# A hybrid decoder layer in fp32: other places in SBUF for up blocks' weights and for some activations

## The chip, the core and the metric

The kernel runs on one core of a Trainium2 chip. The metric is the time on the device in microseconds (us); each number of "runs" is a median over executions that were timed one by one. One further execution was profiled, and all rows shown come from it. The engines are TensorE (PE in the rows; its weight loads are PEld), VectorE (DVE), ScalarE (ACT), GpSimd (POOL) and SyncE (SP), which issues the weight DMAs. SBUF is the on-chip memory from which all of them read.

## The reference

One post-norm decoder layer on 256 tokens plus 16 meta tokens, width 2048, all in fp32. Cut to what matters here:

```
p   = h @ w_in                              # q heads, shared latent, indexer, pool channels
mix = concat(attention(p), pooling(p)) @ w_o
h   = LN(alpha * h + mix)
z   = h @ w_up                              # 2048 -> 2 x 5632
a, g = split(causal depthwise conv (width 3) of z)
h   = LN(alpha * h + (gelu(a) * g) @ w_down) # 5632 -> 2048
```

Nearly all of the work is in the four products with `w_in`, `w_o`, `w_up` and `w_down`.

## The kernel before

**Three products for one.** TensorE multiplies operands in the type fp32r. To keep fp32's precision each fp32 operand is cut into an upper and a lower part, and each matmul is done as three: upper weight by upper activation (L288), and the two mixed ones (L292, in a loop). With weights of 128 x 128 and activations of 128 x 258 (256 tokens and two more that the convolution wants) a block of 128 output columns takes 16 K steps of three matmuls. `product` (L281 to 292) is this loop. The order of the two mixed matmuls is `turned` (weight's lower part first) or not.

**The weight stream.** All weight tiles of 128 x 2048 go through one stream (L158 on): `w_in` (tiles `in_w_proj`), the latent's two tiles, `w_o` (16 tiles), then the tiles of the FFN in the order that `ffn_plan` writes down: an up tile and a down tile by turns, 88 up and 80 down, the four last down tiles at the end. The up blocks are numbered b = 2f + half, where half 0 is the value and half 1 the gate of column block f. The first 8 of them work on activations into which LayerNorm is folded (`fold`, 260 columns wide with two extra), the other 80 on normalised activations `hp`, made by `normalise` (L799 to 808). The FFN has six parts of columns; from the second part on a down tile of the part before follows each up tile. A down tile of `seven` (L890 to 892) computes 4 or 3 of the seven products of a 2 x 2 Strassen scheme, kind A or B by turns, with activations `gp` and `right`.

**From DMA to TensorE.** For a tile, `fetch` issues the DMA on SP's queue into a raw tile `wraw`; then `split_part` makes the upper part by a copy on ScalarE (L181) and the lower part by a subtraction on VectorE (L182), both into the tile `whl`. This is done in pieces, given by `cuts`: (0, 1024, 2048), or (0, 512, 2048) where the tile has a lead. A tile of kind A or B has one or three more subtractions on VectorE (L193 to 199). `wraw` and `whl` have three buffers each, and tiles are fetched two ahead of their use. VectorE and ScalarE also do the convolution (L821 to 823), the gate (L838, L839) and the activations' splits, in an order that a scheduler sets from the program's order and its own model; `issue_after` adds edges to it.

**Where the parts stand.** `Split` (L68 to 82) is the layout of a `whl` tile: the upper part at one offset, the lower at another, in elements of 4 bytes. With a **lead**, the first 512 columns (the first four K steps) stand elsewhere: their upper part at the lead's offset, the lower part 576 further on, and the rest behind. `places` and `WAYS` give offsets and turn by position in the stream; `LEAD_X` is the lead of eight tiles of the input projection, `LEAD_H` = (12, False) that of three tiles of `w_o` and of all up tiles (`lead(b)`). Tiles of `w_o` without a lead stand at 0 and 2048, turned; an up tile has this too for the part behind its lead. `Parts` (L85 to 92) is the layout of an activation tile: `xp` (input) at 0 and 274, `hp` at 2 and 276, `fold` at 32 and 304. `K_UP` is the order of K steps in an up block; its first entry is K tile 1.

Of the kernel before, what the change touches and what calls it, by code (L numbers as in the profile page):

```python
# [12 lines left out]
F32R = mybir.dt.float32r  # L13
# [4 lines left out]
P = 128  # L18
# [3 lines left out]
T = NM + S  # L22
Q0 = NM - 2
NQ = T - Q0
# [43 lines left out]
class Split:  # L68

    def __init__(self, tile, upper, lower, turned=False, lead=None, early=False):

        self.tile, self.places, self.turned, self.lead, self.early = tile, (upper, lower), turned, lead, early

    def __getitem__(self, key):
        rows, part, c = key
        o = self.places[part]
        if self.lead is not None:
            assert c.stop <= LEAD or c.start >= LEAD  # L80
            o = self.lead + (LEAD + 64) * part if c.stop <= LEAD else self.places[0] + LEAD + 128 + (2048 - LEAD) * part
        return self.tile[rows, o + c.start:o + (2 * 1024 + 2 if c.stop is None else c.stop)]


# [9 lines left out]


WIDE = 288
LEAD = 512
WAYS = (10, 2048, False), (12, 2048, True), (0, 2048, True), (0, 2048, True)


LEAD_X, LEAD_H = (24, False), (12, False)


def lead(b):

    return LEAD_H


GATED, RIGHT, FOLD = 0, 32, 32
# [20 lines left out]
K_UP = (1, 3, 5, 7, 8, 10, 12, 15, 0, 2, 4, 6, 9, 11, 13, 14)  # L130
# [3 lines left out]
def tile_layer(ctx, tc, xt, w_first, w_proj, w_uk, w_uv, w_pool, w_o, w_up, w_down, cols, rows, rel_bias, onehot, out):  # L134
# [3 lines left out]
    ring = ctx.enter_context(tc.tile_pool(name="ring", bufs=24))  # L138
# [21 lines left out]
    for item in plan:  # L160
# [3 lines left out]
        elif item[0] == "down":  # L164
            n = PARTS[FAST]
# [19 lines left out]
    def fetch(raw, hl, src, kind, front):  # L185

        nc.sync.dma_start(raw, src)
        b11, b12, b21, b22 = (raw[:, c:c + 512] for c in range(0, 2048, 512))
        cuts = (0, 1024, 2048)
        if kind == "A":  # L190

            with tc.issue_after(front):
                nc.vector.tensor_tensor(b12, b12, b11, op=ALU.subtract)  # L193
        if kind == "B":

            with tc.issue_after(front):
                nc.vector.tensor_tensor(b12, b22, b12, op=ALU.subtract)  # L197
            nc.vector.tensor_tensor(b11, b12, b11, op=ALU.add)  # L198
            nc.vector.tensor_tensor(b21, b21, b11, op=ALU.subtract)
            cuts = (0, 1024, 1536)  # L200
        if hl.lead is not None:
            cuts = (0, LEAD, 2048)
        for a, b in zip(cuts, cuts[1:]):
            parts = split_part(raw, hl, slice(a, b))
        return parts
# [75 lines left out]
    def product(ps, hl, act, lo, hi, places, ks=None, k0=0, k1=KT):  # L281

        for n in range(k0, k1):
            k = (places if ks is None else ks)[n]
            w = slice(P * places.index(k), P * places.index(k) + P)
            wh, wl = hl[:, 0, w], hl[:, 1, w]
            ah, al = act[k][:, 0, lo:hi], act[k][:, 1, lo:hi]
            nc.tensor.matmul(ps, wh, ah, start=n == 0, stop=False)  # L288
            turned = hl.early if hl.lead is not None and w.start < LEAD else hl.turned
            turn = ((wl, ah), (wh, al)) if turned else ((wh, al), (wl, ah))  # L290
            for i, (a, b) in enumerate(turn):
                nc.tensor.matmul(ps, a, b, start=False, stop=i == 1 and n == KT - 1)  # L292
# [6 lines left out]
    for k0, k1 in [(k, k + 1) for k in range(9)] + [(9, 12), (12, 15), (15, 16)]:  # L299
        if k0 == KT - 1:  # L300

            raw = ap_.tile([P, 1024], F32, name="wraw_l", tag="v1")[:, :T + MF].rearrange("p (a b) -> p a b", a=1)
        elif k0 % 3 == 0:
            raw = wp.tile([P, 2048], F32, tag="wraw", name="wraw")
            raw = raw[:, :3 * (T + MF)].rearrange("p (a b) -> p a b", b=T + MF)
        if k0 % 6 == 0:
            hl = split_tile()
        for w in ((slice(0, T), slice(T, T + MF)) if k0 == 0 else (slice(0, T + MF),)):
            nc.sync.dma_start(raw[:, k0 % 3:k0 % 3 + k1 - k0, w], w_first[k0:k1, :, w].rearrange("k p c -> p k c"))
        for k in range(k0, k1):  # L310
            xk, wk, a0 = raw[:, k % 3, :T], raw[:, k % 3, T:], k % 6 // 3 * 1024 + k % 3 * MF
            c = slice(a0, a0 + MF)
            a = Parts(ring.tile([P, 2, WIDE], F32R, tag="act", name="xp"), 0, T)
            nc.scalar.activation(a[:, 0, :], xk, AF.Copy)
            nc.scalar.activation(hl[:, 0, c], wk, AF.Copy)
            nc.vector.tensor_tensor(a[:, 1, :], xk, a[:, 0, :].bitcast(F32), op=ALU.subtract)
            nc.vector.tensor_tensor(hl[:, 1, c], wk, hl[:, 0, c].bitcast(F32), op=ALU.subtract)
            x_parts.append(a)
            first.append((hl, c.start))
# [480 lines left out]
    def normalise(m):  # L800
# [1 line left out]
        nc.vector.tensor_tensor(yd, yd, rs, op=ALU.mult)  # L802
        nc.vector.tensor_tensor(yd, yd, m2, op=ALU.add)
        nc.scalar.activation(yd, yd, AF.Identity, bias=col(LN1, 2 * m + 1), scale=col(LN1, 2 * m))
        a = Parts(ring.tile([P, 2, WIDE], F32R, tag="act", name="hp"), 2, NQ)
        nc.scalar.activation(a[:, 0, :NQ], yd, AF.Copy)
        nc.vector.tensor_tensor(a[:, 1, :NQ], yd, a[:, 0, :NQ].bitcast(F32), op=ALU.subtract)
        h_parts.append(a)
# [191 lines left out]
    n = PARTS[-1]  # L1000
# [189 lines left out]
```

## Time and profile before

| what | value |
|---|---|
| median of 3 runs | 1026.68 us (1025.87 to 1028.61) |
| profiled execution | 1027.44 us |
| its span, from the first to the last instruction | 1025.6 us |
| TensorE busy, share of the span | 99% |
| VectorE, ScalarE, GpSimd busy | 87%, 60%, 18% |
| HBM read | 232.50 MB |
| the granted clock of TensorE | 0.997 of full speed |

A group of instructions is told by its line, engine, operation, and the tiles written and read (out<-in); x is a count. Behind the busy time a group's row has the mean duration in ns, then the idle time of the engine ahead of the group and what ended it. A timeline's row has a start in us from the span's begin, a duration in us, and the instruction. Matmuls are pipelined: a next one may start before the one ahead of it ends, so that how long a block takes is read from starts and not from durations. The chain that ended last is followed back from the last instruction, at each step to what released it.

### The profile page before, as it was taken

The page shows a single profiled execution, that of the slowest core. Times are in us where ns is not written, and L with a number is a line of the kernel's source. Part 1 is how long each engine was busy: PE and PEld are TensorE (multiplying, and loading weights), DVE is VectorE, ACT ScalarE, POOL GpSimd, SP SyncE. Part 2 cuts the span into 40 slices and gives each one's busy share as a digit, 9 for nine tenths or more (in the row PEclk, how much of TensorE's full clock was granted, in tenths as well). Part 3 has the DMA queues.
Part 4 walks back from the last instruction along what each step waited for, and adds up shares of the span by engine and source line. Part 5 has one row for each costly group of instructions (what it writes and reads, how often), then busy time and mean ns, then how long its engine had stood idle before and what let it go on. Part 6 is the DMA issues. An engine that isn't in the chain of part 4 may idle for free.

```text
span 1025.6 us, 19201 instructions
## 1 busy us (share of the span) xinstructions
PE 1018.5 (99%) x7644; PEld 969.4 (95%) x7644; DVE 890.5 (87%) x1401; ACT 620.1 (60%) x1000; POOL 188.4 (18%) x245
## 2 busy tenths in 40 slices
PE   9999999999999999999999999999999999999997
PEld 8999999999999999999999999999999999999986
DVE  6878668758879998999998989989899999999876
ACT  7666446645448856555666565566556656666675
POOL 1200014125430131111121111210212102120031
PEclk9999999999999999999999999999999999999998
DMA  8755643455564578979887788888888789788874
GB/s 328 257 184 206 228 154 108 138 197 168 203 205 134 189 229 249 278 283 296 281 288 259 270 275 278 277 279 298 278 272 279 292 295 289 266 290 286 290 244 138
DMA packets 59754, 250.28 MB, mean 244 GB/s; under 512 B 21734, under 2 KB 22416, under 8 KB 32656
## 3 DMA queue, kind: packets, MB, share of 16 engines
q1 hardware_dynamic: 34592, 230.42, 62.8%
q0 software_dynamic: 7888, 16.14, 8.3%
q10 hardware_dynamic: 17184, 2.49, 1.5%
q8 instruction: 60, 0.98, 0.4%
q14 instruction: 30, 0.25, 0.1%
HBM read 232.50 MB, written 2.11 MB: 229 GB/s over the span
## 4 chain that ended last, share of the span: by engine, by line
PE 71%; DVE 12%; DMA 8%; issue 4%; ACT 4%; POOL 1%; POOLq 0%; ACTq 0%; SPq 0%; DVEq 0%
PE mm L292 36%; PE mm L288 18%; DVE whl L182 6%; DMA wraw<-in_w_up 4%; DMA wraw<-in_w_down 4%; ACT whl L181 3%; PE at L891 3%; PE at L892 3%; PE at L890 3%; PE mm L363 2%; DVE y L900 1%; DVE wraw L198 1%; DVE wraw L197 1%; DVE gp L845 0%; DVE wraw L193 0%
## 5 line engine op out<-in xcount | busy, mean ns | idle before, releaser
L182 DVE TENSOR_TENSOR whl<-wraw,whl 128x1024 fp32r<-128x1024 f32 (+2 forms) x416 | 488.3, 1201 | 53.8 <-ACT whl L181 52.4
L181 ACT ACTIVATE whl<-wraw 128x1024 fp32r<-128x1024 f32 (+2 forms) x416 | 402.4, 1015 | 192.8 <-DVE wraw L198 52.1
L292 PE MATMUL mm<-hp,whl 128*128 128x258 f32 x2560 | 454.0, 280 | 0.0
L292 PEld LDWEIGHTS mm<-hp,whl 128*128 128x128 f32 x2560 | 390.9, 188 | 3.5 <-DVE whl L182 0.2
L288 PE MATMUL mm<-hp,whl 128*128 128x258 f32 x1280 | 357.6, 279 | 0.0
L288 PEld LDWEIGHTS mm<-hp,whl 128*128 128x128 f32 x1280 | 241.4, 189 | 3.1
L292 PE MATMUL mm<-xp,whl 128*128 128x256 f32 (+5 forms) x768 | 140.4, 282 | 0.0
L292 PEld LDWEIGHTS mm<-xp,whl 128*128 128x128 f32 x768 | 118.7, 189 | 0.5
L288 PE MATMUL mm<-xp,whl 128*128 128x256 f32 (+5 forms) x384 | 111.9, 292 | 0.0
L863 POOL TENSOR_TENSOR forms<-za 128x128 f32<-128x128 f32 x20 | 20.3, 1015 | 297.5 <-DVE za L839 234.5
L288 PEld LDWEIGHTS mm<-xp,whl 128*128 128x128 f32 x384 | 72.3, 188 | 1.0 <-issue 0.5
L891 PE MATMUL at<-whl,gp 128*128 128x512 f32 x180 | 70.7, 393 | 0.0
L892 PE MATMUL at<-whl,gp 128*128 128x512 f32 x180 | 70.6, 393 | 0.0
L890 PE MATMUL at<-whl,gp 128*128 128x512 f32 x180 | 68.8, 392 | 0.3 <-DVE u L914 0.3
L866 POOL TENSOR_TENSOR forms<-za 128x128 f32<-128x128 f32 x20 | 20.2, 1010 | 202.3 <-DVE za L839 190.2
L821 ACT ACTIVATE z<-mm,cv 128x256 f32<-128x256 f32 x40 | 22.3, 559 | 42.5 <-PE mm L292 42.2
L292 PE MATMUL mm<-fold,whl 128*128 128x260 f32 x256 | 45.6, 280 | 0.0
L292 PE MATMUL mm<-mixp,whl 128*128 128x258 f32 x256 | 45.5, 279 | 0.0
L292 PE MATMUL mm<-mixa,whl 128*128 128x258 f32 x256 | 45.2, 278 | 0.0
L821 ACT ACTIVATE za<-mm,cv 128x256 f32<-128x256 f32 x40 | 22.3, 558 | 35.0 <-PE mm L292 33.8
L892 PEld LDWEIGHTS at<-whl,gp 128*128 128x128 f32 x180 | 33.8, 188 | 7.4
L890 PEld LDWEIGHTS at<-whl,gp 128*128 128x128 f32 x180 | 33.5, 187 | 7.2 <-DVE u L914 1.0
(339 smaller groups left out, 1610.1 us busy)
## 6 DMA issues: line engine op xcount, KB each, us to landing
wraw<-in_w_up SPq DMA_DIRECT2D x88, 1024.0 KB, 5.2
wraw<-in_w_down SPq DMA_DIRECT2D x80, 1024.0 KB, 6.5
wraw<-in_w_proj SPq DMA_DIRECT2D x24, 1024.0 KB, 5.2
wraw<-in_w_o SPq DMA_DIRECT2D x16, 1024.0 KB, 4.9
y<-v POOLq DMA_DIRECT2D x27, 256.0 KB, 8.4
y<-u POOLq DMA_DIRECT2D x18, 256.0 KB, 5.0
wraw<-in_w_first SPq DMA_DIRECT2D x8, 304.0 KB, 5.2
x<-in_xt SPq DMA_DIRECT2D x1, 2176.0 KB, 7.8
```

What stands on the lines that cost most here:

```text
L181: upper = nc.scalar.activation(hl[:, 0, c], raw[:, c], AF.Copy)
L182: lower = nc.vector.tensor_tensor(hl[:, 1, c], raw[:, c], hl[:, 0, c].bitcast(F32), op=ALU.subtract)
L197: nc.vector.tensor_tensor(b12, b22, b12, op=ALU.subtract)
L288: nc.tensor.matmul(ps, wh, ah, start=n == 0, stop=False)
L292: nc.tensor.matmul(ps, a, b, start=False, stop=i == 1 and n == KT - 1)
L363: nc.tensor.matmul(ps[:m, :T], hl[:, t // 2, a0 + a:a0 + a + m], x_parts[k][:, t % 2, :], start=k == 0 and t == 0, stop=k == KT - 1 and t ...
L821: nc.scalar.activation(z, src[:, 2:NQ], AF.Identity, bias=col(C_B, j), scale=col(C_W, 3 * j + 2))
L863: nc.gpsimd.tensor_tensor(s[:, 0], a21, a22, op=ALU.add)
L866: nc.gpsimd.tensor_tensor(s[:, 3], a11, a21, op=ALU.subtract)
L890: nc.tensor.matmul(ps, a[:, 0, i], hl[:, 0, w], start=j == 0, stop=False)
L891: nc.tensor.matmul(ps, a[:, 0, i], hl[:, 1, w], start=False, stop=False)
L892: nc.tensor.matmul(ps, a[:, 1, i], hl[:, 0, w], start=False, stop=j == n - 1)
```

## The change

Three things, all of them offsets in SBUF and what hangs on them.

1. A lead's length is now a number of K steps, given with it. Up blocks 0 to 7 keep theirs of four steps. Blocks 8 to 16 have five (`KEPT`). Blocks from 17 on, which are 71 of 88, have none: their tile stands at 0 and 2048, turned from the first step on, and is split in pieces of 1024 and 1024 columns.
2. The `hp` tile that an up block takes first (K tile 1) stands at 22 and 296 in place of 2 and 276 (`ASIDE`).
3. The input activations `xp` stand at 20 and 294 in place of 0 and 274, and so do the weights of the input projection, by 20 elements, lead included. The weights of the first product (latent, indexer keys; L363) stay.

```diff
@@ -69,16 +69,17 @@
 
 
 
-    def __init__(self, tile, upper, lower, turned=False, lead=None, early=False):
-
-        self.tile, self.places, self.turned, self.lead, self.early = tile, (upper, lower), turned, lead, early
+    def __init__(self, tile, upper, lower, turned=False, lead=None, early=False, steps=0):
+
+        self.tile, self.places, self.turned, self.lead, self.early, self.first = tile, (upper, lower), turned, lead, early, P * steps
 
     def __getitem__(self, key):
         rows, part, c = key
         o = self.places[part]
         if self.lead is not None:
-            assert c.stop <= LEAD or c.start >= LEAD
-            o = self.lead + (LEAD + 64) * part if c.stop <= LEAD else self.places[0] + LEAD + 128 + (2048 - LEAD) * part
+            n = self.first
+            assert c.stop <= n or c.start >= n
+            o = self.lead + (n + 64) * part if c.stop <= n else self.places[0] + n + 128 + (2048 - n) * part
         return self.tile[rows, o + c.start:o + (2 * 1024 + 2 if c.stop is None else c.stop)]
 
 
@@ -94,16 +95,17 @@
 
 
 WIDE = 288
-LEAD = 512
-WAYS = (10, 2048, False), (12, 2048, True), (0, 2048, True), (0, 2048, True)
-
-
-LEAD_X, LEAD_H = (24, False), (12, False)
+WAYS = ((30, 2048, False), (32, 2048, True), (0, 2048, True), (0, 2048, True))
+
+
+LEAD_X, LEAD_H, KEPT, ASIDE = (44, False, 4), (12, False, 4), (12, False, 5), 20
 
 
 def lead(b):
 
-    return LEAD_H
+    if b < 8:
+        return LEAD_H
+    return KEPT if b <= 16 else ()
 
 
 GATED, RIGHT, FOLD = 0, 32, 32
@@ -199,7 +201,7 @@
             nc.vector.tensor_tensor(b21, b21, b11, op=ALU.subtract)
             cuts = (0, 1024, 1536)
         if hl.lead is not None:
-            cuts = (0, LEAD, 2048)
+            cuts = (0, hl.first, 2048)
         for a, b in zip(cuts, cuts[1:]):
             parts = split_part(raw, hl, slice(a, b))
         return parts
@@ -286,7 +288,7 @@
             wh, wl = hl[:, 0, w], hl[:, 1, w]
             ah, al = act[k][:, 0, lo:hi], act[k][:, 1, lo:hi]
             nc.tensor.matmul(ps, wh, ah, start=n == 0, stop=False)
-            turned = hl.early if hl.lead is not None and w.start < LEAD else hl.turned
+            turned = hl.early if hl.lead is not None and w.start < hl.first else hl.turned
             turn = ((wl, ah), (wh, al)) if turned else ((wh, al), (wl, ah))
             for i, (a, b) in enumerate(turn):
                 nc.tensor.matmul(ps, a, b, start=False, stop=i == 1 and n == KT - 1)
@@ -310,7 +312,7 @@
         for k in range(k0, k1):
             xk, wk, a0 = raw[:, k % 3, :T], raw[:, k % 3, T:], k % 6 // 3 * 1024 + k % 3 * MF
             c = slice(a0, a0 + MF)
-            a = Parts(ring.tile([P, 2, WIDE], F32R, tag="act", name="xp"), 0, T)
+            a = Parts(ring.tile([P, 2, WIDE], F32R, tag="act", name="xp"), 20, T)
             nc.scalar.activation(a[:, 0, :], xk, AF.Copy)
             nc.scalar.activation(hl[:, 0, c], wk, AF.Copy)
             nc.vector.tensor_tensor(a[:, 1, :], xk, a[:, 0, :].bitcast(F32), op=ALU.subtract)
@@ -802,7 +804,7 @@
         nc.vector.tensor_tensor(yd, yd, rs, op=ALU.mult)
         nc.vector.tensor_tensor(yd, yd, m2, op=ALU.add)
         nc.scalar.activation(yd, yd, AF.Identity, bias=col(LN1, 2 * m + 1), scale=col(LN1, 2 * m))
-        a = Parts(ring.tile([P, 2, WIDE], F32R, tag="act", name="hp"), 2, NQ)
+        a = Parts(ring.tile([P, 2, WIDE], F32R, tag="act", name="hp"), 2 + (ASIDE if m == K_UP[0] else 0), NQ)
         nc.scalar.activation(a[:, 0, :NQ], yd, AF.Copy)
         nc.vector.tensor_tensor(a[:, 1, :NQ], yd, a[:, 0, :NQ].bitcast(F32), op=ALU.subtract)
         h_parts.append(a)
```

The number of matmuls is the same. The lines of the changed kernel are those of the kernel before plus 2 behind L94.

On TensorE the order of instructions changes at three places, all in the FFN's second part, where the first down tiles (`at`) are used and an up block's first matmuls (`mm<-hp`) stand ahead of a down block's last ones. The first of them, in the kernel before:

```order
L892 MATMUL at<-whl,gp 128x512
L891 MATMUL at<-whl,gp 128x512
L892 MATMUL at<-whl,gp 128x512
L288 MATMUL mm<-hp,whl 128x258
L292 MATMUL mm<-hp,whl 128x258
L891 MATMUL at<-whl,gp 128x512
L892 MATMUL at<-whl,gp 128x512
L891 MATMUL at<-whl,gp 128x512
L892 MATMUL at<-whl,gp 128x512
L292 MATMUL mm<-hp,whl 128x258
L288 MATMUL mm<-hp,whl 128x258
L292 MATMUL mm<-hp,whl 128x258 x2
```

and in the changed one:

```order
L894 MATMUL at<-whl,gp 128x512
L893 MATMUL at<-whl,gp 128x512
L894 MATMUL at<-whl,gp 128x512
L290 MATMUL mm<-hp,whl 128x258
L893 MATMUL at<-whl,gp 128x512
L894 MATMUL at<-whl,gp 128x512
L893 MATMUL at<-whl,gp 128x512
L894 MATMUL at<-whl,gp 128x512
L294 MATMUL mm<-hp,whl 128x258 x2
L290 MATMUL mm<-hp,whl 128x258
L294 MATMUL mm<-hp,whl 128x258 x2
```

Two of the up block's matmuls stood ahead of the down block's last four, and now one does. At the second place it is likewise, and at the third two became none. The down block's matmuls are the same.

On VectorE the order of the FFN's middle, at one of seven places that read alike: the end of one convolution (`za`), the pieces of the weight splits (`whl`), the extra subtraction of a down tile (L193), the next convolution (`z`) and the gate (L839). Before:

```order
L822 SCALAR_TENSOR_TENSOR za<-mm,cv,za 128x256
L823 SCALAR_TENSOR_TENSOR za<-mm,cv,za 128x256
L182 TENSOR_TENSOR whl<-wraw,whl 128x1024
L182 TENSOR_TENSOR whl<-wraw,whl 128x512 x2
L182 TENSOR_TENSOR whl<-wraw,whl 128x1536
L193 TENSOR_TENSOR wraw<-wraw 128x512
L822 SCALAR_TENSOR_TENSOR z<-mm,cv,z 128x256
L823 SCALAR_TENSOR_TENSOR z<-mm,cv,z 128x256
L182 TENSOR_TENSOR whl<-wraw,whl 128x1024
L839 TENSOR_TENSOR za<-za,z 128x256
L182 TENSOR_TENSOR whl<-wraw,whl 128x1024
```

After:

```order
L824 SCALAR_TENSOR_TENSOR za<-mm,cv,za 128x256
L825 SCALAR_TENSOR_TENSOR za<-mm,cv,za 128x256
L184 TENSOR_TENSOR whl<-wraw,whl 128x1024
L184 TENSOR_TENSOR whl<-wraw,whl 128x512
L184 TENSOR_TENSOR whl<-wraw,whl 128x1024 x2
L195 TENSOR_TENSOR wraw<-wraw 128x512
L824 SCALAR_TENSOR_TENSOR z<-mm,cv,z 128x256
L825 SCALAR_TENSOR_TENSOR z<-mm,cv,z 128x256
L184 TENSOR_TENSOR whl<-wraw,whl 128x1024
L841 TENSOR_TENSOR za<-za,z 128x256
L184 TENSOR_TENSOR whl<-wraw,whl 128x1024
```

The up tile's pieces of 512 and 1536 columns are now two of 1024; the pieces of 1024 and 512 beside them belong to down tiles. Nothing else changes its place here. The orders on GpSimd and on SP's queue are the same.

## Rows read from the trace of the kernel before

**Rows 1.** The page's busy and chain lines; busy times of 390 to 975 us

```profile
PE 1018.5 (99%) x7644; PEld 969.4 (95%) x7644; DVE 890.5 (87%) x1401; ACT 620.1 (60%) x1000; POOL 188.4 (18%) x245
PE 71%; DVE 12%; DMA 8%; issue 4%; ACT 4%; POOL 1%; POOLq 0%; ACTq 0%; SPq 0%; DVEq 0%
390.00:975.00 585.00, 584.57 (x4235) 550.55 (x4234) 543.01 (x742) 352.61 (x494) 91.82 (x109) 1.00 0.85 281
```

**Rows 2.** TensorE's timeline, a usual up block (start, duration in us)

```profile
683.25 0.28 PE L288 MATMUL mm<-hp,whl 128*128 128x258 f32 x1
...
684.68 0.28 PE L288 MATMUL mm<-hp,whl 128*128 128x258 f32 x1
...
685.75 0.28 PE L288 MATMUL mm<-hp,whl 128*128 128x258 f32 x1
...
688.87 0.39 PE L890 MATMUL at<-whl,right 128*128 128x512 f32 x1
```

**Rows 3.** TensorE's timeline, first and last start of ten output projection blocks

```profile
243.00 0.28 PE L288 MATMUL mm<-mixp,whl 128*128 128x258 f32 x1
...
298.47 0.28 PE L288 MATMUL mm<-fold,whl 128*128 128x260 f32 x1
```

**Rows 4.** TensorE's timeline, part of an up block, 426 to 430 us

```profile
426.96 0.29 PE L288 MATMUL mm<-hp,whl 128*128 128x258 f32 x1
...
430.26 0.39 PE L890 MATMUL at<-whl,right 128*128 128x512 f32 x1
```

**Rows 5.** TensorE's timeline, one up block and one down block

```profile
642.37 0.28 PE L288 MATMUL mm<-hp,whl 128*128 128x258 f32 x1
642.65 0.50 PE L292 MATMUL mm<-hp,whl 128*128 128x258 f32 x2
...
644.43 0.29 PE L288 MATMUL mm<-hp,whl 128*128 128x258 f32 x1
...
647.00 0.39 PE L890 MATMUL at<-whl,right 128*128 128x512 f32 x1
...
760.90 0.40 PE L890 MATMUL at<-whl,right 128*128 128x512 f32 x1
761.42 0.50 PE L891 MATMUL at<-whl,right 128*128 128x512 f32 x1
761.75 0.40 PE L892 MATMUL at<-whl,right 128*128 128x512 f32 x1
```

**Rows 6.** Groups by line and form, 390 to 975 us, VectorE and ScalarE

```profile
L182 DVE TENSOR_TENSOR whl<-wraw,whl 128x1024 fp32r<-128x1024 f32 x111 | 134.0, 1222 | 5.6 <-ACT whl L181 5.1
L182 DVE TENSOR_TENSOR whl<-wraw,whl 128x1536 fp32r<-128x1536 f32 x71 | 125.9, 1774 | 10.8 <-ACT whl L181 10.4
L182 DVE TENSOR_TENSOR whl<-wraw,whl 128x512 fp32r<-128x512 f32 x107 | 73.8, 704 | 6.0 <-ACT whl L181 5.9
...
L181 ACT ACTIVATE whl<-wraw 128x1024 fp32r<-128x1024 f32 x112 | 115.4, 1056 | 117.1 <-DVE wraw L198 52.1 <-DVE wraw L193 40.0 <-issue 13.1
L181 ACT ACTIVATE whl<-wraw 128x512 fp32r<-128x512 f32 x107 | 65.3, 623 | 28.7 <-DMA wraw<-in_w_up 27.5 <-PE at L892 1.1
```

**Rows 7.** The chain that ended last, 630 to 650 us (start, duration, what)

```profile
631.43 7.26 DMA wraw<-in_w_up
...
638.79 2.02 ACT whl L181 x2
...
640.84 1.76 DVE whl L182
```

**Rows 8.** Timelines of VectorE and of TensorE near 787 us

```profile
786.09 2.35 DVE L182 TENSOR_TENSOR whl<-wraw,whl 128x512 fp32r<-128x512 f32 x2
...
787.21 0.28 PE L288 MATMUL mm<-hp,whl 128*128 128x258 f32 x1
```

**Rows 9.** TensorE's timeline, an input projection block and the next one's start

```profile
109.56 0.28 PE L288 MATMUL mm<-xp,whl 128*128 128x258 f32 x1
...
115.28 0.28 PE L288 MATMUL mm<-xp,whl 128*128 128x258 f32 x1
```

## The prediction

> **What bounds the kernel now.** I read the page first: its lines of busy time and of the chain that ended last. TensorE is busy for 99% of the span, and 71% of the chain is TensorE; most of the rest is the feed of weights (DMA, ScalarE, VectorE) [rows 1]. So two things can move the time: how close together TensorE's matmuls start, and the few places where the feed is late. A busy share says nothing about the first, so next I read TensorE's timeline, block by block, by start times. One K step of a block is three matmuls, one at L288 and two at L292; I call the time from one L288 start to the next a beat.
>
> A usual up block of the middle of the FFN starts at 683.25 us and the next kind of block at 688.87, so it takes 5.62 us. Its first four beats, those of the lead, take 683.25 to 684.68, 1.43 us or 0.3575 each; three more, to 685.75, take 1.07 or 0.357 each; the last nine take 3.12 or 0.3467 each [rows 2]. All have the same shape, 128x258. The output projection has ten blocks in a row without a lead, from 243.00 to 298.47 us: 5.547 each, which is 16 beats of 0.3467 [rows 3]. These blocks have the offsets that the changed kernel gives its up blocks: weights at 0 and 2048 elements, activations at 2 and 276, the same order of the three. A third rate is seen in the same shape and at the same offsets: from 426.96 to 430.26 us nine beats take 3.30, 0.3667 each [rows 4]. So where the operands stand, and how a block was entered, sets the beat: good 0.3467, lead 0.3575, slow 0.3667.
>
> **Up blocks from number 17 on.** These are 71 of the 88. Lead removed: the best that it can give is a block of 5.547 in place of 5.62, 0.073 saved, 71 x 0.073 = 5.2 us. The other end within the good case: the first K step, whose activations now stand at 22 and 296, takes a lead's beat of 0.3575, three beats settle as they do behind a lead (1.07), and twelve are good (12 x 0.3467 = 4.16), together 5.588; that saves 0.032 a block, 2.3 us. I take the middle, 3.7 us.
>
> Why expect the good beat at all? Behind a down block the usual block's lead goes into the good beat [rows 2], and a block entered after a wait went into the slow one [rows 5, 4]. The code gives a reason to think that the moved K step stands in for a lead: in the lead the activations start 2 - 12 and 276 - 12 elements from the weights, in the moved step 22 - 0 and 296 - 0. Counted modulo 32 elements these are 22 and 8 both times. That only differences modulo 128 bytes count is an assumption; no row shows it.
>
> The Trainium skill, page "SBUF — State Buffer", section "Who interferes with whom", says that TensorE has two independent read ports (moving operand and weights) and that "PE and ACT never wait on anyone". By that, operand places could not matter and this term would be zero. The trace disagrees: one shape, three rates, 0.3467, 0.3575 and 0.3667 us for three matmuls [rows 2 to 4]. What hangs on the rule is a rival below.
>
> **Starts in the first down blocks.** In the first down part the first one or two matmuls of an up block stand ahead of a down block's last ones. At three of these places the order on TensorE changes: two ahead become one or none. The work is the same, so only the beat behind it can change. The block with the slow beat at 426.96 us is one of those with one ahead, which stays [rows 4]. Taken at zero; if the slow beat of one block came or went there, sixteen beats at 0.02, it would be 0.3 us either way.
>
> **The cuts of the split.** Without a lead a tile is split in 1024 + 1024 columns, not 512 + 1536. VectorE's pieces take 1.222 against 0.704 and 1.774 us [rows 6]: twice 1.222 is 2.444 against 2.478, so the sum is the same, and VectorE, busy for 543 of 585 us there [rows 1], gets no relief in work. What moves is when each part is ready. The second part's last step is 0.55 shorter, and it is wanted at step 8 and not at step 4, four beats later: 1.4 us more cover. In the chain that ended last a tile lands at 638.69, ScalarE takes 2.02 for both parts and VectorE 1.76 for the second, and TensorE, at step 4 of a block, starts matmuls at 642.37 and 642.65 where 0.12 would be usual: 0.16 lost [rows 5, 7]. The block then stays slow for most of its rest. That wait and its tail, about 0.4 with eleven beats at 0.02, should go. Against that, the first part is ready about 0.52 later by VectorE alone, up to 0.95 with ScalarE's longer piece (1.056 against some 0.62). The tightest place that I found: VectorE starts the piece of 512 at 786.09, has it at about 786.8, and the block starts at 787.21 [rows 8]; a cover of 0.4, so there a wait of 0.1 to 0.5 may come. The worst wait is in a down block: 760.90 to 761.42 to 761.75, 0.52 and 0.33 where 0.23 is usual, 0.4 lost [rows 5]. Its own cuts don't change, but the feed ahead of it has shorter last steps. Bounds for all of this: 0.8 gained (both waits gone) to 1.2 lost (the up blocks' gain of some twenty blocks between two tight places eaten by the feed, 20 x 0.052, and a new wait of 0.2). I take 0.5 gained, nearer to the first, since the chain's rows are the ones that get shorter.
>
> **Blocks 8 to 16.** Their lead grows from four steps to five: one beat more at 0.3575 in place of a good one, at most 0.011 x 9 = 0.1 us lost. If the moved first step spoils their lead, they go slow: 9 x 16 x 0.02 less what the lead costs, at most 2.5 us.
>
> **The first activations.** In the input projection activations and weights move by the same 20 elements, so each difference stays. Taken at zero. The blocks there are not on the good beat: one of the eight with 258 columns lasts from 109.56 to 115.28, 5.72 us [rows 9]. Should absolute places count, sixteen such blocks have 5.72 - 5.547 = 0.173 each to win, 2.8 us, or 16 x 0.3667 = 5.867, 0.147 each, to lose, 2.4 us. The first product (latent, keys) has activations that move against weights that don't; it is some 48 beats, at 0.02 one us either way, also taken at zero.
>
> **The sum.** -3.7 - 0.5 + 0.1 = -4.1 us. The profiled execution took 1027.44 us (span 1025.6 and 1.8 around it), 0.8 over the median of the three runs, 1026.68. So 1023.3 for such an execution, 1022.6 against the median. I forecast 1022.6.
>
> **Rivals.**
> Places don't matter, or the blocks take a beat between good and lead with no gain: then only the cuts and blocks 8 to 16 count, -0.4: 1026.3. The rule of the skill's page comes to the same time. Against it stand [rows 2, 3], the same shape at two rates without a wait. For it: nothing behind a down block ever ran without a lead here, so the entry is untested. Chance 0.13.
>
> The feed eats the gain: TensorE would run 0.05 faster per block while VectorE at 93% keeps its work, and each tight place becomes a wait. Of the 3.7 some 2 are left, less the rest: 1025. For it: 24% of the chain, some 240 us, is DMA, ScalarE and VectorE [rows 1]; against it: the cuts shorten that chain. Chance 0.08.
>
> Slower, by one mechanism: without a lead the block enters on the slow beat and stays there, as the block at 426.96 did from its eighth step to its end, lead or no lead [rows 4]. Each such block costs 5.867 - 5.62 = 0.247. Up blocks stand behind two kinds of down block by turns; if one kind gives a slow entry, 36 x 0.247 - 35 x 0.052 = 7.1 more, less 0.4 for the rest: 1033.4. If both do, 71 x 0.247 = 17.5 more: 1043.8. It decides from about 15 slow blocks on (15 x 0.247 against 71 x 0.052). For it: the blocks that entered the good offsets after a disturbance [rows 4, 5] went slow. Against it: the differences of the moved step. Chances 0.10 and 0.08.
>
> **How the numbers follow.** The forecast has 0.61; its own range, with the ends of its terms (-5.2 - 0.8 and half of the first activations' gain at one end, -2.3 and +0.6 at the other), is 1019.3 to 1025.0. What a measurement of this kernel can tell from no change is about 0.3%, 3.1 us, so faster begins below 1023.6: some five sixths of the forecast's share, 0.50, and little else, 0.52 in all. Same: 0.11 of the forecast, and most of the first two rivals, 0.29. Slower: the slow beat, and blocks 8 to 16 or the first activations gone wrong beside a lost gain, 0.19. The range of 1019.3 to 1031.5 leaves out the two slow cases and little below.
>
> **What would show it.** Right: up blocks of the middle at 5.55 to 5.59 us from first matmul to the next block's, with beats of 0.347 from the fifth step at the latest; no gap at step 4 of a block near 640 us; VectorE's busy time unchanged; blocks of the input projection still at 5.72. Wrong: beats of 0.353 or 0.367 to a block's end, up blocks at 5.65 or 5.87; the first matmul of an up block waiting for VectorE's first part; input blocks far from 5.72 in either direction.

## The result, and the profile after

The changed kernel takes 1034.95 us (median of 4 runs, 1032.55 to 1035.74) against 1026.47 before: a ratio of the means of 1.0075, 95% interval 1.0052 to 1.0097. It is slower, where 1022.6 was forecast. The profiled execution took 1034.49 us with a span of 1032.7, 7.1 more than the span of before; its stretches below add up to that.

The first thing to see is which chain ended last. The page's line on engines, of the changed kernel:

```profile
PE 89%; DVE 5%; issue 3%; ACT 1%; DMA 1%; POOL 1%; POOLq 0%; SPq 0%; DVEq 0%; ACTq 0%
```

TensorE has gone from 71% [rows 1] to 89%, and DMA, VectorE and ScalarE from 24% to 7%. In this trace no matmul of an up or a `seven` block from block 17 on starts late for its feed; in the trace of the kernel before such waits came to 1.3 us. That the change took them away does not follow. One of the runs below moves the first activations and leaves the FFN as it was before, and its trace has none of these waits either. Its page:

```profile
PE 94%; issue 2%; DMA 1%; DVE 1%; POOL 1%; ACT 0%; SPq 0%; POOLq 0%; DVEq 0%; ACTq 0%
```

So the share of the feed in [rows 1] belongs to that execution; what the change altered from block 17 on is TensorE's own pace.

The pace is read from starts, as before. TensorE's timeline of the changed kernel: two up blocks without a lead and the start of the down block behind each, then a block of the input projection and three starts in the output projection:

```profile
476.66 0.28 PE L290 MATMUL mm<-hp,whl 128*128 128x258 f32 x1
...
477.02 0.28 PE L290 MATMUL mm<-hp,whl 128*128 128x258 f32 x1
...
477.38 0.28 PE L290 MATMUL mm<-hp,whl 128*128 128x258 f32 x1
...
477.73 0.29 PE L290 MATMUL mm<-hp,whl 128*128 128x258 f32 x1
...
482.50 0.40 PE L892 MATMUL at<-whl,gp 128*128 128x512 f32 x1
...
517.03 0.28 PE L290 MATMUL mm<-hp,whl 128*128 128x258 f32 x1
...
517.38 0.28 PE L290 MATMUL mm<-hp,whl 128*128 128x258 f32 x1
...
517.73 0.28 PE L290 MATMUL mm<-hp,whl 128*128 128x258 f32 x1
...
522.59 0.39 PE L892 MATMUL at<-whl,right 128*128 128x512 f32 x1
...
102.83 0.28 PE L290 MATMUL mm<-xp,whl 128*128 128x258 f32 x1
...
108.45 0.28 PE L290 MATMUL mm<-xp,whl 128*128 128x258 f32 x1
...
218.84 0.29 PE L290 MATMUL mm<-mixp,whl 128*128 128x258 f32 x1
...
224.70 0.29 PE L290 MATMUL mm<-mixp,whl 128*128 128x258 f32 x1
...
230.57 0.29 PE L290 MATMUL mm<-mixp,whl 128*128 128x258 f32 x1
```

The first block stands between two down blocks of kind A (the next one starts with `gp`): 5.84 us to the down block, where the usual block of before took 5.62 [rows 2]. Its first three beats are 0.36, 0.36 and 0.35; the other 13, from 477.73 on, take 4.77, 0.367 each, the slow beat of [rows 4]. The second block stands between two of kind B (`right` next): 5.56; two beats of 0.35, and from 517.73 on 14 in 4.86, 0.347 each. This repeats four and four to the end. Of the 71 blocks 32 take 5.83, all behind kind A, and 37 take 5.56 to 5.60; the other two take 5.67. The four other blocks behind kind A, in the first down part, are not slow (5.56 to 5.67).

The input block takes 5.62, not 5.72 [rows 9]. The output projection's blocks 2 and 3, counted from 0 as its weight tiles are, take 5.86 and 5.87 here, the slow beat throughout, and so does block 4; the same three took 5.547 before, and the ten blocks of [rows 3] take 5.547 in both kernels. Two expectations below call them blocks 1 to 3; block 1 is on the slow beat from its seventh step on.

The other loss lies where the first blocks on `hp` wait. TensorE's timeline there, with what it waited for in brackets (us and releaser):

```profile
351.28 0.39 PE L290 MATMUL mm<-hp,whl 128*128 128x258 f32 x1 [0.35 <-ACT hp L808]
351.51 0.28 PE L294 MATMUL mm<-hp,whl 128*128 128x258 f32 x1
353.19 0.58 PE L294 MATMUL mm<-hp,whl 128*128 128x258 f32 x1 [1.40 <-DVE hp L809]
353.56 0.42 PE L290 MATMUL mm<-hp,whl 128*128 128x258 f32 x1
...
354.21 0.42 PE L290 MATMUL mm<-hp,whl 128*128 128x258 f32 x1
```

VectorE's timeline of the same time, changed kernel:

```profile
348.58 0.41 DVE L809 TENSOR_TENSOR hp<-x,hp 128x258 fp32r<-128x258 f32 x1
...
350.44 2.35 DVE L184 TENSOR_TENSOR whl<-wraw,whl 128x640 fp32r<-128x640 f32 x2
352.71 0.42 DVE L809 TENSOR_TENSOR hp<-x,hp 128x258 fp32r<-128x258 f32 x1
```

and of the kernel before:

```profile
348.04 1.75 DVE L182 TENSOR_TENSOR whl<-wraw,whl 128x1536 fp32r<-128x1536 f32 x1
349.71 0.77 DVE L807 TENSOR_TENSOR hp<-x,hp 128x258 fp32r<-128x258 f32 x2
```

Before, the last two activation tiles follow each other, done by 350.5. In the changed kernel the split of one more weight tile (2.35 us) stands ahead of the last, which is done at 353.1, and TensorE waits for it in block 8's last two steps. What it costs further is in the table by stretch of the changed kernel (us; the last three columns are TensorE's granted clock, DMA's share and GB/s):

```profile
350.00:353.50 3.50, 1.75 (x11) 1.33 (x10) 3.47 (x7) 1.23 (x3) 0.00 (x0) 0.94 0.66 267
353.50:357.00 3.50, 3.50 (x19) 3.50 (x19) 2.83 (x6) 3.50 (x7) 1.44 (x3) 0.57 0.89 300
357.00:361.00 4.00, 4.00 (x35) 4.00 (x34) 4.00 (x8) 2.52 (x7) 1.35 (x3) 1.00 0.06 12
```

TensorE was busy for half of the first stretch; behind it the granted clock is 0.57, so most of that stretch ran at the lower level, 1.2 and not 2.4 GHz, and beats take 0.65 (353.56 to 354.21) until full speed is back near 356.7.

The 7.1 us by stretches, each from the difference of block starts in the two traces: the input projection and what is ahead of it -1.6 (1.2 of it in the projection's blocks; the rest lies ahead of its first block, whose start varies from 22.6 to 23.7 us between the traces); the output projection's blocks 1 to 4 +1.1; blocks 8 and 9 +4.1; the slow tail of blocks 10 to 16 +1.1 (7 x 0.16); blocks from 17 on with their down blocks +2.5; the end -0.1. Of the +4.1 some 3.7 is the late activation tile (2.4 of waiting in block 8 and 1.3 at the lower clock in block 9), the rest the slow beat. The +2.5 is +4.0 in the up blocks (sum of 71: 404.1 against 400.1) and -1.5 beside them, of which 1.0 is waits in the down blocks of the kernel before. The waits of before, the lower clock and the output projection's blocks are not the same in every execution, as the runs below show, so the 7.1 is that of these two executions.

### The profile page after: what moved, and what is told of

It is laid out like the page before. It is cut to its first block, busy times and chain, and to the rows that moved or that the text cites. A ratio compares the mean times of both kernels' runs of the same rounds, so it can differ in the third digit from the quotient of the medians.

```text
span 1032.7 us, 19200 instructions
## 1 busy us (share of the span) xinstructions
PE 1023.4 (99%) x7644; PEld 976.2 (95%) x7644; DVE 891.0 (86%) x1401; ACT 621.3 (60%) x1000; POOL 192.9 (19%) x245
## 4 chain that ended last, share of the span: by engine, by line
PE 89%; DVE 5%; issue 3%; ACT 1%; DMA 1%; POOL 1%; POOLq 0%; SPq 0%; DVEq 0%; ACTq 0%
PE mm L294 44%; PE mm L290 22%; PE at L892 6%; PE at L893 6%; PE at L894 6%; PE mm L365 2%; DVE whl L184 2%; DMA wraw<-in_w_down 1%; ACT whl L183 1%; DVE hp L809 0%; DVE x L804 0%; POOL gb L1011 0%; PE mm L593 0%; PE at L454 0%; PE at L628 0%
## 5 line engine op out<-in xcount | busy, mean ns | idle before, releaser
L184 DVE TENSOR_TENSOR whl<-wraw,whl 128x1024 fp32r<-128x1024 f32 (+4 forms) x416 | 486.2, 1202 | 38.4 <-ACT whl L183 37.3
L183 ACT ACTIVATE whl<-wraw 128x1024 fp32r<-128x1024 f32 (+4 forms) x416 | 402.0, 1014 | 105.7 <-PE mm L294 24.7
L294 PE MATMUL mm<-hp,whl 128*128 128x258 f32 x2560 | 461.0, 281 | 1.4 <-DVE hp L809 1.4
L290 PE MATMUL mm<-hp,whl 128*128 128x258 f32 x1280 | 363.0, 284 | 0.4 <-ACT hp L808 0.4
L823 ACT ACTIVATE z<-mm,cv 128x256 f32<-128x256 f32 x40 | 22.6, 566 | 95.4 <-PE mm L294 95.4
L865 POOL TENSOR_TENSOR forms<-za 128x128 f32<-128x128 f32 x20 | 21.1, 1055 | 302.7 <-DVE za L841 236.6
L823 ACT ACTIVATE za<-mm,cv 128x256 f32<-128x256 f32 x40 | 22.6, 565 | 79.4 <-PE mm L294 79.4
L868 POOL TENSOR_TENSOR forms<-za 128x128 f32<-128x128 f32 x20 | 24.9, 1246 | 200.1 <-DVE za L841 180.8
```

What stands on the lines that cost most here:

```text
L183: upper = nc.scalar.activation(hl[:, 0, c], raw[:, c], AF.Copy)
L184: lower = nc.vector.tensor_tensor(hl[:, 1, c], raw[:, c], hl[:, 0, c].bitcast(F32), op=ALU.subtract)
L823: nc.scalar.activation(z, src[:, 2:NQ], AF.Identity, bias=col(C_B, j), scale=col(C_W, 3 * j + 2))
L865: nc.gpsimd.tensor_tensor(s[:, 0], a21, a22, op=ALU.add)
L868: nc.gpsimd.tensor_tensor(s[:, 3], a11, a21, op=ALU.subtract)
```

## The experiments

All are built on the changed kernel unless said otherwise, and were run beside the kernel before (medians 1026.85 to 1027.00 in those runs).

**The lead of five steps.**

```diff
-... KEPT, ASIDE = (44, False, 4), (12, False, 4), (12, False, 5), 20
+... KEPT, ASIDE = (44, False, 4), (12, False, 4), (12, False, 4), 20
```

> The changed kernel, but blocks 8 to 16 keep a lead of four steps (pieces of 512 and 1536 columns), which puts the order on VectorE around the last activation tiles back to that of before. Theory: the five-step lead moved one more weight tile's split (2.3 us) ahead of the last hp tile, TensorE waited 2.4 us for it near 351 us and then ran 1.5 us longer at the half clock; so the waits at 351 to 357 us go and the time falls by 4.0 us, to about 1031.0. Blocks 9 to 16 stay slow (5.78 us each) because their first step is the moved one. Rival: the length of the lead made those blocks slow, then they return to 5.62 and it falls by 5.2. Other rival: the wait has to do with the moved activations, then nothing changes.

1031.1 us, 1.0040 (1.0023 to 1.0057): as expected. The wait and the low clock are gone, and the blocks are still slow. TensorE's timeline, block 9 (first matmul and that of the next):

```profile
352.01 0.29 PE L290 MATMUL mm<-hp,whl 128*128 128x258 f32 x1
...
357.81 0.29 PE L290 MATMUL mm<-hp,whl 128*128 128x258 f32 x1
```

5.80, not 5.62. So the late tile came from the cuts of the five-step lead, through the order on VectorE; the slow tail did not.

**The moved step taken back.**

```diff
-... (12, False, 5), 20
+... (12, False, 5), 0
```

> The changed kernel with the first K tile's activations back at 2 and 276; blocks from 17 on still without a lead, blocks 8 to 16 with five steps. Theory: the moved step is what lets a block without a lead enter on the good beat behind a kind B down block; without it all 71 are slow, 5.83 to 5.87 us, some 9.7 us more, while blocks 9 to 16 return to about 5.63 (1.2 us less): a span of about 1041. Rival: the kind of the down block alone decides (slow behind A, good behind B), then the pattern stays and only the 1.2 us go: 1031.5.

1043.74 (one run), span 1042.0. All but four of the 71 blocks are slow, behind A 5.86, behind B 5.83. The same place as the slow block above:

```profile
476.45 0.28 PE L290 MATMUL mm<-hp,whl 128*128 128x258 f32 x1
...
482.31 0.40 PE L892 MATMUL at<-whl,gp 128*128 128x512 f32 x1
```

Blocks 10 to 16 go back to 5.63. So the moved activations give the good beat behind kind B, and spoil a lead at 12. The rival, that the kind alone decides, falls.

**Only the first activations.** The kernel before with `xp` at 20 and the projection's weights 20 further on, nothing else.

> The kernel before with only the shift of the first activations and of the input projection's weights by 20 elements; leads of all up blocks and the place of hp as before. Theory: the input projection gains what it gained in the changed kernel, 1.6 us by 130 us of the span (0.10 for a block of 258 columns, 0.067 for one of 256), and the output projection's blocks 1 to 3 go slow again (1.1 us more), as they do in the changed kernel; up blocks at 5.62: 0.5 us less than before, 1026.0. Rival: the slow output projection blocks came from something later in the change; then 1.6 less, 1024.9.

1025.92, 0.9988 (0.9972 to 1.0005). In its trace the input blocks take 5.62, as forecast, and the output projection's blocks 2 to 4 5.87, as forecast too, but that came by chance: with the same instructions up to there they are good in most of the later runs. The net gain of 1 us can't be told from none by its interval. The cuts of the split are those of before, and yet the block that waited near 642 us takes its 5.62 and the down block that waited at 760.90 [rows 5] has 0.23 from start to start:

```profile
760.13 0.39 PE L892 MATMUL at<-whl,right 128*128 128x512 f32 x1
760.36 0.39 PE L893 MATMUL at<-whl,right 128*128 128x512 f32 x1
760.59 0.39 PE L894 MATMUL at<-whl,right 128*128 128x512 f32 x1
```

**Where kind A's weights stand.**

```diff
-    return (0, 2080) if kind == "A" else (48, 2112)
+    return (48, 2112)
```

> The changed kernel with the weights of kind A down tiles at the places of kind B (48 and 2112 in place of 0 and 2080). Theory 1: where the down block's weights stand decides how the next up block is entered; then the blocks behind A enter as those behind B, 5.56 in place of 5.83, some 33 x 0.27 = 8.8 us less: a span of about 1024. Theory 2: it is something else of kind A (four products of three matmuls against three, or which activations come last); then the pattern of four slow and four good blocks stays and the time changes by under 1 us.

1025.76 (one run), span 1023.9. Theory 1 holds. A block between two of kind A, and one between two of kind B:

```profile
474.21 0.28 PE L290 MATMUL mm<-hp,whl 128*128 128x258 f32 x1
...
479.80 0.39 PE L892 MATMUL at<-whl,gp 128*128 128x512 f32 x1
...
513.83 0.28 PE L290 MATMUL mm<-hp,whl 128*128 128x258 f32 x1
...
519.39 0.39 PE L892 MATMUL at<-whl,right 128*128 128x512 f32 x1
```

5.59 and 5.56: no block from 17 on is slow any more (three of them, from 698 us on, take 5.66).

**The two places exchanged**, A at 48, B at 0.

> The changed kernel with the places of the two kinds exchanged: A at 48 and 2112, B at 0 and 2080. Theory: the place decides and the kind does not, so now the blocks behind B are slow (5.83) and those behind A good (5.59 as with both at 48): the span near the changed kernel's, 1031 to 1033. Rival: kind B gives the good entry at any place, then all blocks are good and the span is about 1024.

1032.64 (one run), span 1030.9. Behind A, then behind B:

```profile
474.81 0.28 PE L290 MATMUL mm<-hp,whl 128*128 128x258 f32 x1
...
480.40 0.39 PE L892 MATMUL at<-whl,gp 128*128 128x512 f32 x1
...
506.93 0.28 PE L290 MATMUL mm<-hp,whl 128*128 128x258 f32 x1
...
512.77 0.40 PE L892 MATMUL at<-whl,right 128*128 128x512 f32 x1
```

5.59 and 5.84. The slow entry has moved from A to B with the offsets, and the rival falls: the offsets of the down block's weights decide, not its kind. It is not quite the same picture: the first block of each four behind B takes 5.67, and only the other three are slow.

**Kind A at 16 and 2096, and at 112 and 2176.**

> The changed kernel with kind A's weights at 16 and 2096 elements in place of 0 and 2080; 16 and 48 are the same place counted modulo 32 elements (128 bytes), and 16 is not the place of kind B. Theory: places count modulo 128 bytes, then blocks behind A enter as with 48, 5.594, and the span is within 1 us of 1023.9. Rival: some longer period or the equality with B's places counts, then they stay slow at 5.83 or take a rate of their own: 1030 to 1033.

> The changed kernel with kind A's weights at 112 and 2176: 64 elements (256 bytes) on from 48 and 2112, and not the same as B's. Theory: places count modulo 256 bytes (modulo 128 bytes is refuted by 16), so blocks behind A enter as with 48: 5.594, a span of 1023 to 1026 with the late activation tile's wait still in. Rival: only the very places of B do, or a longer period counts; then 5.83 or a rate of its own, 1030 or more.

At 16: 1034.95 (one run), span 1033.2; at 112: 1024.71 (one run), span 1022.8. The block behind A, at 16:

```profile
475.93 0.28 PE L290 MATMUL mm<-hp,whl 128*128 128x258 f32 x1
...
481.76 0.40 PE L892 MATMUL at<-whl,gp 128*128 128x512 f32 x1
```

5.83, slow. But this run doesn't test the first theory as its expectation has it: 16 is 48 less 32 elements, while the lower part went from 2112 to 2096, by 16 elements, and so is not at the same place counted modulo 32. Whether places 128 bytes apart are alike for down blocks stays open. At 112 and 2176 both parts stand 64 elements (256 bytes) on from 48 and 2112:

```profile
474.25 0.28 PE L290 MATMUL mm<-hp,whl 128*128 128x258 f32 x1
...
479.85 0.39 PE L892 MATMUL at<-whl,gp 128*128 128x512 f32 x1
```

5.60 by these rows; the blocks take 5.59 behind A and 5.56 behind B, as with 48, and the second theory held. One rival is left by all of these runs: where the block behind is slow (0 and 2080, 16 and 2096) the two parts are 2080 elements apart, and where it is good (48 and 2112, 112 and 2176) 2064. Whether the upper part's place, the lower part's or their distance decides, no run separates.

**A lead at 44 in place of 12** (up blocks from 8 on, activations not moved, leads of four steps everywhere).

> The kernel before with the shift of the first activations, and with the lead of up blocks from 8 on at 44 in place of 12 elements (32 further on, the same place modulo 128 bytes); activations at 2 and 276, four steps, all as before otherwise. If places count modulo 128 bytes, as the prediction assumed for up blocks, nothing changes: 5.624 a block with four first beats of 0.3575 to 0.360, 1026. Theory: they count modulo 256 bytes, as the two runs on kind A's places say; then the lead has another beat, and up blocks take another time than 5.62, most likely the slow tail (5.78 to 5.83, 80 x 0.17 = 13 us more, 1039) or a good entry (5.56, 1021).

1033.03 (one run), span 1031.2. Two blocks behind down blocks:

```profile
464.94 0.28 PE L290 MATMUL mm<-hp,whl 128*128 128x258 f32 x1
...
470.76 0.40 PE L892 MATMUL at<-whl,gp 128*128 128x512 f32 x1
...
473.51 0.28 PE L290 MATMUL mm<-hp,whl 128*128 128x258 f32 x1
...
479.21 0.40 PE L892 MATMUL at<-whl,gp 128*128 128x512 f32 x1
```

5.82 and 5.70, where a lead at 12 gave 5.62 [rows 2]. Here both parts of the lead moved by 32 elements, so for the lead of an up block 128 bytes more are another place; of the runs this alone tests it. Neither the slow tail nor the good entry came throughout, as I had thought likeliest; blocks take 5.62, 5.69 or 5.81 by turns.

**No lead from block 8 on, kind A at 48.** `lead(b)` returns `()` from block 8.

> The changed kernel with kind A's weights at 48 and 2112 as well, and no lead from block 8 on (the lead of five steps is gone, all tiles from block 8 on are split 1024 and 1024). Theory: the late activation tile's wait and the half clock behind it go (3.9 us less than with kind A's places alone, 1025.8), and blocks 8 to 16, each behind another up block on the good beat, stay on it with the moved first step, 5.56 in place of 5.78, 9 x 0.22 = 2.0 less: 1019.9, 0.993 of the kernel before. Rival: only a down block at 48 gives the good entry, and blocks that follow each other go slow, 5.85: 1022.4.

1023.49, 0.9963 (0.9951 to 0.9976): faster than both kernels, but 3.6 us above the expectation: the theory was half wrong. Its blocks 8 to 16, which follow each other with no down block between, go round three paces, 5.56, 5.66 and 5.84, and a wait for the last activation tile is still there, if a shorter one:

```profile
351.24 0.39 PE L290 MATMUL mm<-hp,whl 128*128 128x258 f32 x1 [1.00 <-ACT hp L808]
...
351.93 0.39 PE L294 MATMUL mm<-hp,whl 128*128 128x258 f32 x1 [0.18 <-DVE hp L809]
```

**The same with a lead in the output projection's block 2.**

> As the kernel without leads from block 8 on and with kind A's weights at 48, and a lead also for the output projection's block 2. Blocks 1 to 3 there are on the good beat in some executions (5.55) and on the slow one in others (5.87), with the same instructions. Theory: a lead brings the beat back to good whatever the state ahead of it, so blocks 2 to 4 are good in each: in executions that were slow there 0.7 us are saved, in the others 0.07 lost; the median falls by 0.3 at most, and the spread shrinks. Rival: the state comes from further back and the lead doesn't mend it: no difference.

1024.45, 0.9976 (0.9963 to 0.9988): no better than without. In the profiled executions of both versions these blocks were on the good beat, so nothing was tested there but the lead's cost of 0.07. Inconclusive.

**The same with cuts of 512 and 1536** for tiles without a lead, places unchanged.

> The kernel with no lead from block 8 on and kind A's weights at 48, with the same places, but its up tiles are split 512 and 1536 as before, not 1024 and 1024. Theory 1: the cuts set the scheduler's order, so the wait of 1.7 us near 351 us goes; and the cuts are also what took away the waits at step 4 of a block and in the down blocks (1.3 us in the kernel before), so waits of that kind come back: 1.3 or more. Together within 0.5 of 1023.5. Theory 2: those waits went for another reason, then only the wait near 351 goes: 1021.8.

1022.24, 0.9956 (0.9943 to 0.9970). The wait for the activation tile is gone: the cuts set that order. Of waits for the feed one came back, in a down block:

```profile
781.53 0.39 PE L896 MATMUL at<-whl,gp 128*128 128x512 f32 x1
782.04 0.50 PE L894 MATMUL at<-whl,gp 128*128 128x512 f32 x1
782.38 0.40 PE L895 MATMUL at<-whl,gp 128*128 128x512 f32 x1
```

0.4 us, not 1.3. The time lies between those of the two theories, and its interval (1021.0 to 1023.8) holds both. Nor does the wait that came back settle it: of the four traces with the old cuts from block 17 on, this one and that of the kernel before have such waits, and those with only the first activations moved and with the lead at 44 have none; of the ten with the new cuts none has one of over 0.05 us. The cuts may make such waits rarer; that they took away those of the kernel before is not shown.

**The moved tile fifth.** Kind A at 48, four-step leads for blocks 8 to 16; the moved activations are those of K tile 8, fifth in the tile, and blocks from 17 on take it first:

```diff
+    moved_first = [K_UP[4]] + [k for k in K_UP if k != K_UP[4]]
...
-... 2 + (ASIDE if m == K_UP[0] else 0), NQ)
+... 2 + (ASIDE if m == K_UP[4] else 0), NQ)
...
-... ks=late_last if f == FOLDED else None)
+... ks=late_last if f == FOLDED else moved_first if 2 * f + half_ > 16 else None)
```

> Kind A's weights at 48 and 2112; blocks from 17 on without a lead, but the moved activations are those of the K tile that stands fifth in the weight tile (K tile 8), and blocks from 17 on take it first. Blocks 8 to 16 have their lead of four steps and take the moved tile as fifth step, with weights at 0. Theory: there it is one more step of a lead, so these blocks take 5.63 (as with a five-step lead and unmoved activations); the order on VectorE is that of before around the last activation tiles, so no wait near 351 us; blocks from 17 on as with the moved first step, 5.56 and 5.59. Against the kernel with no lead from block 8 on, 1023.5: 1.7 less for the wait, 0.4 less for the blocks: 1021.4, 0.995 of the kernel before. Rival: the moved fifth step throws blocks 8 to 16 onto the slow beat: 1022.5.

1022.75, 0.9960 (0.9947 to 0.9974). No wait near 351; blocks 8 to 16 one after the other:

```profile
350.29 0.29 PE L290 MATMUL mm<-hp,whl 128*128 128x258 f32 x1
...
355.99 0.29 PE L290 MATMUL mm<-hp,whl 128*128 128x258 f32 x1
```

5.70: neither the 5.63 of the theory nor the slow 5.79. This version and the one before it are the fastest of the study, some 0.4% faster than the kernel before, and not told apart.

## Why the prediction was wrong

**The step that failed** is the entry of blocks from 17 on: "the moved K step stands in for a lead". Behind kind B it does (5.56, the middle of the two ends that the term had); behind kind A it does not, save in the first down part. The term was -3.7; the up blocks measure +4.0: 32 blocks on the slow beat at 0.209 each are +6.7, the rest gained. The rival that one kind of down block gives a slow entry, with a chance of 0.10, had the right mechanism and condition. That its time, 1033.4, came near is luck: its term for the up blocks was +7.1, and the late tile and the tail of blocks 10 to 16, which it did not have, made up the rest. The assumption beneath the step, that only differences modulo 128 bytes count, was marked as resting on no row, and it carried the forecast all the same; the lead at 44 refutes it for the lead of up blocks. Counted modulo 64 elements (256 bytes) the differences are 54 and 8 in the lead and 22 and 40 in the moved step, and not alike. (The part of an up tile behind its lead, put above at 0 and 2048, stands 640 and 128 elements on from these, both multiples of 64.) What the runs show in its place: the offsets of the down block's weights set the entry of the block behind it (5.83 behind 0 and 2080, 5.56 to 5.59 behind 48 and 2112, whichever kind stands there, with the first of each four behind B at 0 taking 5.67), and offsets 256 bytes apart were alike in the one pair that was run.

**The cuts of the split** were looked at for blocks from 17 on alone. For blocks 8 to 16 only the beat was counted, "at most 0.011 x 9 = 0.1", and not that other cuts are another order on VectorE: the last `hp` tile went behind one more split, and that is +3.7, half of the slowdown of the profiled execution; the lead of four steps took it away. For blocks from 17 on the term of -0.5 was priced from waits of one execution. The waits at 642 and 760 are gone, and one at 655 that I had not seen, 1.3 in all; but they are gone as well with the old cuts and only the first activations moved. So no run shows that the cuts gain anything there. The wait at 642 was also read too short: by the start of the step behind it 0.26 was lost and not 0.16, and 0.45 with the slow tail, against the 0.4 that was summed.

**Blocks 8 to 16.** "If the moved first step spoils their lead, they go slow" was the bound, at most 2.5; seven of them measure 1.1, and all nine 1.5 where the late tile is out of the way (the lead of four steps). The bound should have been the value: in the lead the weights stand at 12, not at 0, so by the argument's own differences the moved step did not match there.

**The first activations** were taken at zero because each difference stays. The blocks gain 1.2, inside the bounds of -2.8 to +2.4. That speaks for absolute places, unless the blocks inherit their pace from the first product, whose differences did change; no run separates the two. **The starts in the first down blocks** came to nothing that can be told.

**Not foreseen**: the output projection's blocks 2 to 4. In 13 profiled executions with the same instructions up to there, the changed kernel's and the twelve runs' (one has a lead at block 2), they were slow in four and good in nine: 1.1 us that comes and goes. One thing differs ahead of them: the first beat of block 1, longer than usual in every trace, is 0.442 to 0.445 us in those four traces and 0.449 to 0.455 in the nine others and the kernel before. What makes this difference, and whether it is the cause, is not shown.

The Trainium skill's rule that "PE and ACT never wait on anyone" (page "SBUF — State Buffer", section "Who interferes with whom") was read in the prediction as saying that operand places cannot matter. That reading, one of the rivals, fell: with 16 and 2096 for 48 and 2112 in one kind of tile and nothing else, the two spans differ by 9.3 us (1.1 of it in the output projection's blocks), and no wait in the profile explains it. Whether TensorE ever waits for another engine's access to SBUF, of which the rule speaks, no run here tests.

What stays open is why these places matter. That the offsets of one block's operands set the beat of the next is shown; which of its two parts, or their distance, and what in the memory does it was not measured.

## What to carry to other kernels

When a matmul engine is busy for 99% and the feed is on time, look at starts: blocks of one shape can run at several paces, and a block can inherit its pace from the operands of the block ahead, so try a new placement behind each kind of block that can precede it. An assumption that no row shows should not carry the sign of a forecast: price its failure first. A wait seen in one execution may be that execution's own: look for it in a second one before it becomes a term. To test a period of places, move every part of a tile by that period. And where a change alters the sizes of pieces that a scheduler orders, compare the order of everything else on that engine, not only of the pieces.

## What the runs showed of the hardware that was not expected

- Three matmuls of 128x258 settle at 0.347, 0.353 or 0.367 us, by the places of the operands and by how a block is entered (three output projection blocks took 5.55 or 5.87 each at the same places), and stay there until something disturbs them: whole blocks at 5.55, 5.66 and 5.87. Moving a lead by 128 bytes (12 to 44) took blocks from 5.62 to 5.62, 5.69 or 5.81 by turns. Moving one kind of down tile by 256 bytes (48 to 112) left the blocks behind it at 5.59; with that tile at 0 or 16 they took 5.83.
- The wait for the late activation tile was followed by the lower clock in two of the six profiled executions that had the five-step lead's order (in the changed kernel's granted 0.57 over 3.5 us, beats of 0.65); in the other four the next block ran at full speed. The wait over the last two steps was 2.40 and 2.44 us in the two and 2.30 to 2.34 in the four. The price of one late tile was so 2.3 us, or 3.7 to 4.0.
